# Mixer A's queries and keys projected for four heads at a time

## The chip, the cores and the metric

The kernel runs on one core of a Trainium2 chip. The metric is the device time of one execution in microseconds (us). Five engines take part: TensorE (PE, matmuls and transposes, with its own weight loads PEld), VectorE (DVE), ScalarE (ACT), GpSimd (POOL) and SyncE (SP), which here issues nearly every DMA. Each engine works through its own list of instructions in order; semaphores tie the lists together.

## The reference, cut to what matters

One layer of a streaming encoder, run for 1024 prompt frames and 32 sample frames with shared weights. The kernel puts them side by side as T = 1056 rows of x with 1024 channels: nine tiles of rows, eight of 128 and one of 32. What the change touches is the first lines of `project_inputs`:

```
h = rmsnorm(x, g_mix)
z = einsum('bld,de->ble', h, w_in)
q_a, k_a, v_a, q_i, k_i, w_i, q_b, k_b, v_b, gate_a, gate_b = split(z, ...)
q_a = rope(rmsnorm(q_a.reshape(B, L, 8, 64), g_qn), pos)    # 8 heads of 64
k_a = rope(rmsnorm(k_a.reshape(B, L, 8, 64), g_kn), pos)    # also an output
```

Mixer A (sparse attention over the 256 keys that an indexer picks) uses these queries and keys; mixer B (stick-breaking attention) has its own. Gates, an output projection and a feed-forward block follow. All of it is float32; the kernel reaches that accuracy by splitting each operand into a high and a low float32r part and adding three products (high by high, high by low, low by high).

## The kernel before, in words

All instructions are recorded first and put in order by a planner (`Plan`): each has a rank (FAST, PREP, MAIN, FILL, SLOW) and an estimated duration, and the planner walks a clock over the five engines, giving each engine next the ready instruction of the best rank, the earlier recorded one first. Since every instruction is issued by the planner, all of them carry one line, L408, in the profile; groups are told apart by their tiles. Names end in numbers in the order lists; the profile leaves these out.

The stage that changes begins at about 279 us and ends when the attention of the first heads starts, at about 488 us. In it stand:

- `project_a(p)`, rank MAIN, for p = 0 to 3, two heads at a time: 256 columns of weights (128 of queries, 128 of keys). Four weight blocks (`w_qka[p, j]`, 128 x 512 each, holding two channel blocks of 256 columns) are loaded into `wst`, cast to the high part `wh` on ACT and subtracted to the low part `wl` on POOL. For each tile of rows s, 24 matmuls (8 channel blocks k by 3 products) put 128 x 256 into a bank `s` of PSUM, of which there are three; x is the stationary operand, the weights move. ACT squares the bank into `sq`, DVE sums it into `ss`, and DVE multiplies the bank by the rope tables `tabc` and `tabs` into `ta` and `tb`, which POOL adds into `qk`. After all nine tiles comes a chain of small DVE operations (`f`, `rv`, `rw`) for the norms, then transposes of `qk` into banks `t`, their split into `az`, and stores to DRAM (`dq`, `dk`, and the output `out_k_a`).
- `project_v(p)`, inside `project_a`: two weight blocks `w_va`, 72 matmuls of rank FILL into banks `pj` (chunks of 512, 272 and 272 columns), a scaling to `vt`, transposes, and stores `dv`.
- `gate(e)` for e = 2, 3, 4 (`w_g`, 72 FILL matmuls each, scaled to `gz`, stored to `dg`).
- the top-k search of the indexer, rank SLOW, on DVE and ACT: rounds of counting (`junk`, `cnta`, `cntb` from `score` and `cand`) and, at its end, the masks (`pen`, `eq`, `pre`, `mask`).

FILL matmuls take PE whenever no MAIN matmul is ready. The weight blocks of all of these share one ring of five `wh`/`wl` pairs (WB) and three `wst`: a block can only be cast when PE is through with the block five before it. Four blocks of `w_qka[0]` are loaded ahead (`early`), while gates 0 and 1 run. `rope_tables` loads two rope tables (`ropec`, `ropes`) and multiplies them by the two norm weights into `tabc` and `tabs`, each `[128, 9, 2, 64]`.

Of the kernel before, what the change touches and what calls it, by code (L numbers as in the profile page):

```python
# [416 lines left out]
class Layer:  # L417
# [15 lines left out]
    def unit(self, src):  # L433

        nc = self.nc
        key = (src.tensor.name, src.offset)
        if key in self.begun:
            return self.begun.pop(key)
        with nc.rank(PREP):
            st = nc.tile(self.wpool, [128, 512], F32, "wst", bufs=3)  # L440
            h = nc.tile(self.wpool, [128, 512], F32R, "wh", bufs=WB)
            l = nc.tile(self.wpool, [128, 512], F32R, "wl", bufs=WB)
            nc.sync.dma_start(st, src)
            self.split(h, l, st)
# [50 lines left out]
    def run(self):  # L495
# [80 lines left out]
        for p in range(4):  # L576
            self.project_a(p)
# [356 lines left out]
    def rope_tables(self):  # L934
# [15 lines left out]

# [51 lines left out]
    def project_a(self, p):  # L1002
        nc, pr, a = self.nc, self.pr, self.a
        units = [self.unit(a["w_qka"][p, j]) for j in range(4)]
        qk = nc.tile(pr, [128, NT, 4, HD], F32, "qk", bufs=1)
        ss = nc.tile(pr, [128, NT, 4], F32, "ss", bufs=2)
        nc.gpsimd.memset(qk[:, NEW], 0.0)
        nc.gpsimd.memset(ss[:, NEW], 0.0)
        for s in range(NT):
# [3 lines left out]
            for k in range(KB):  # L1013
                xh, xl = self.x_of(k, ts_)
                wh, wl = (u[:, (k % 2) * 256:(k % 2) * 256 + 256] for u in units[k // 2])
                nc.tensor.matmul(ps[:m, :256], xh, wh, start=k == 0, stop=False)
                nc.tensor.matmul(ps[:m, :256], xh, wl, start=False, stop=False)
                nc.tensor.matmul(ps[:m, :256], xl, wh, start=False, stop=k == KB - 1)
            sq = nc.tile(pr, [128, 4, HD], F32, "sq", bufs=1)
            if p < SUMS:  # L1020
                nc.scalar.activation(sq[:m], ps[:m, :256].rearrange("p (h e) -> p h e", e=HD), AF.Square)
                nc.vector.reduce_sum(ss[:m, s], sq[:m], axis=AX.X)
            else:
                for h in range(4):
                    nc.scalar.activation(
# [595 lines left out]
```

## Time and profile before

| | us |
|---|---|
| median of 3 timed runs | 1769.09 (1766.96 to 1771.07) |
| profiled execution, first to last instruction (span) | 1767.0 |
| PE busy in it | 1739.5 |
| the stage from 279 to 488 us: PE busy | 207.27 of 209.00 |
| the same: DVE, ACT, POOL busy | 182.41, 127.33, 83.11 |

The profiled execution is as long as the fastest timed run, 1766.96, so nothing of note lies around its span. Durations of matmuls in the profile overlap (they are pipelined); how long one takes out of PE's time is read from the starts of a row of equal ones.

### The profile page before, as it was taken

What the parts mean: (1) busy time and instruction counts of PE and PEld (TensorE: products, weight loads), DVE (VectorE), ACT (ScalarE), POOL (GpSimd) and SP (SyncE); (2) the same over time, 40 slices, a digit from 0 to 9 for tenths busy, and PEclk for the clock granted to TensorE, in tenths of its full rate; (3) what the DMA queues carried; (4) which work ended last, traced back from release to release, by engine and by line L of the source; (5) the groups of instructions that cost most, each with busy time, mean ns of one, the idle gap of its engine ahead of it and who ended that gap; (6) DMA issues with size and microseconds to landing.
All of it is one profiled execution on the core that took longest, in us unless ns stands there. A gap on an engine that the chain in (4) does not pass through costs nothing.

```text
span 1767.0 us, 32459 instructions
## 1 busy us (share of the span) xinstructions
PE 1739.5 (98%) x11394; PEld 1600.1 (91%) x11394; DVE 1175.5 (67%) x2427; ACT 932.7 (53%) x2007; POOL 1054.6 (60%) x901
## 2 busy tenths in 40 slices
PE   8999999999999999999999999999999999999999
PEld 7999999999899888888888888888899999999999
DVE  7555678999666645788975556333357897777764
ACT  7444598973255676766655545432236543333331
POOL 3623232435366574899875555675558986666663
PEclk9999999999999999999999999999999999999999
DMA  8244451544566668555254353433374333333312
GB/s 258 72 133 118 116 177 59 148 144 143 178 179 168 169 183 225 175 163 151 69 162 123 118 154 98 144 109 99 106 237 137 95 104 92 94 91 96 96 48 88
DMA packets 152851, 234.90 MB, mean 133 GB/s; under 512 B 27248, under 2 KB 54480, under 8 KB 152688
## 3 DMA queue, kind: packets, MB, share of 16 engines
q1 hardware_dynamic: 152256, 232.48, 45.8%
q8 instruction: 90, 1.47, 0.4%
q14 instruction: 73, 0.60, 0.1%
q10 hardware_dynamic: 432, 0.34, 0.1%
HBM read 182.58 MB, written 50.08 MB: 132 GB/s over the span
## 4 chain that ended last, share of the span: by engine, by line
PE 85%; DVE 6%; DMA 4%; POOL 3%; issue 1%; ACT 1%; SPq 0%; ACTq 0%; POOLq 0%; DVEq 0%
PE pj L408 53%; PE s L408 13%; PE pd L408 10%; PE t L408 4%; PE o L408 4%; DMA q<-dq 1%; POOL wl L408 1%; DVE xl L408 1%; DMA k<-dk 1%; DVE raw L408 1%; DVE acc L408 1%; DVE rw L408 0%; DMA o<-do 0%; SPq L408 0%; POOL acc L408 0%
## 5 line engine op out<-in xcount | busy, mean ns | idle before, releaser
L408 POOL TENSOR_TENSOR wl<-wst,wh 128x512 fp32r<-128x512 f32 x350 | 488.5, 1400 | 388.4 <-ACT wh L408 358.2
L408 PE MATMUL pj<-xh,wh 128*128 128x512 f32 (+1 forms) x1600 | 557.3, 348 | 0.6 <-DVE vt L408 0.3
L408 PE MATMUL pj<-xh,wl 128*128 128x512 f32 (+1 forms) x1600 | 557.4, 349 | 0.0
L408 PE MATMUL pj<-xl,wh 128*128 128x512 f32 (+1 forms) x1600 | 555.8, 348 | 0.0
L408 ACT CAST wh<-wst 128x512 fp32r<-128x512 f32 x350 | 216.8, 621 | 361.7 <-PE pj L408 222.0
L408 PEld LDWEIGHTS pj<-xh,wh 128*128 128x128 f32 x1600 | 301.1, 188 | 33.6 <-ACT xh L408 0.7
L408 PEld LDWEIGHTS pj<-xh,wl 128*128 128x128 f32 x1600 | 300.8, 188 | 32.7
L408 PEld LDWEIGHTS pj<-xl,wh 128*128 128x128 f32 x1600 | 301.0, 188 | 32.1
L408 PE MATMUL pd<-xh,wh 128*128 128x272 f32 x512 | 147.6, 288 | 2.0 <-DVE y L408 2.0
L408 PE MATMUL pd<-xl,wh 128*128 128x272 f32 x512 | 147.7, 288 | 0.0
L408 PE MATMUL pd<-xh,wl 128*128 128x272 f32 x512 | 147.6, 288 | 0.0
L408 DVE TENSOR_TENSOR xl<-ru,xh 128x272 fp32r<-128x272 f32 (+1 forms) x96 | 114.2, 1202 | 46.0 <-ACT xh L408 45.7
L408 DVE TENSOR_TENSOR tt<-t,tt 128x512 fp32r<-128x512 f32 (+2 forms) x168 | 100.2, 622 | 40.3 <-ACT tt L408 38.6
L408 DVE TENSOR_TENSOR_SCAN rem<-rem 128x896 f32<-128x896 f32 (+6 forms) x66 | 118.7, 1823 | 10.0 <-ACT rem L408 9.8
L408 POOL TENSOR_TENSOR p<-p,rem 128x895 f32<-128x895 f32 (+6 forms) x66 | 103.3, 1578 | 29.8 <-DVE rem L408 26.4
L408 ACT ACTIVATE junk<-score,cand 128x384 bf16<-128x384 f32 (+1 forms) x124 | 116.1, 936 | 9.3 <-DVE cand L408 7.0
L408 ACT CAST tt<-t 128x512 fp32r<-128x512 f32 (+2 forms) x168 | 84.8, 540 | 48.2 <-PE t L408 42.8
L408 DVE TENSOR_TENSOR y<-pj,y 128x512 f32<-128x512 f32 x72 | 49.6, 689 | 83.9 <-PE pj L408 83.8
L408 PE MATMUL s<-k,q 128*128 128x384 f32 (+5 forms) x384 | 95.7, 356 | 7.1 <-DMA k<-dk 2.5
L408 PE MATMUL s<-wl,xh 128*128 128x256 f32 (+1 forms) x360 | 101.8, 285 | 0.2 <-POOL wl L408 0.2
L408 PEld LDWEIGHTS o<-tt,v 128*128 128x128 f32 x640 | 93.0, 189 | 9.7 <-DVE tt L408 1.1
L408 PE MATMUL s<-wh,xh 128*128 128x256 f32 (+1 forms) x360 | 100.3, 286 | 0.9 <-DVE small L408 0.7
(245 smaller groups left out, 3963.6 us busy)
## 6 DMA issues: line engine op xcount, KB each, us to landing
wst<-w_down SPq DMA_DIRECT2D x128, 256.0 KB, 2.7
q<-dq SPq DMA_DIRECT2D x64, 256.0 KB, 5.2
wst<-w_up SPq DMA_DIRECT2D x64, 256.0 KB, 2.7
raw<-w_up SPq DMA_DIRECT2D x64, 256.0 KB, 2.8
k<-dk SPq DMA_DIRECT2D x48, 256.0 KB, 3.5
v<-dv SPq DMA_DIRECT2D x48, 256.0 KB, 3.7
wst<-w_g SPq DMA_DIRECT2D x42, 256.0 KB, 3.4
dv<-vs SPq DMA_DIRECT2D x32, 256.0 KB, 2.4
```

What stands on the lines that cost most here:

```text
L408: fn(*args, **kw)
```

## The change: what it does

`project_a` runs for p = 0 and 1, four heads at a time. Its weights come as eight blocks of 128 x 512, one for each k, holding 256 columns of queries and 256 of keys. The first four use the ring of five; the last four have a ring of their own of four pairs in the pool `proja`, which is opened when the pools of the stage before are closed. Each matmul moves 512 columns and fills a whole bank `s`. `sq`, `ta`, `tb`, `qk`, `ss` and the norm chain are twice as wide and there are half as many. The sum of squares goes by ACT and a DVE sum for all eight columns of heads where p = 0; where p = 1 so for four of them, and for the other four by ACT alone with an accumulating output, as p = 3 did before. The two `project_v` of a pass stand behind the transposes of the first and of the second pair of heads. The rope tables are loaded straight into `tabc` and `tabs`, once for each norm weight, and multiplied in place.

Where the change moves instructions, three places. The first is PE at the start of the stage, where the eight blocks are first used; `s_3785`, `s_3789`, `s_3793` are the banks of row tiles 0, 1 and 2, `wh_1860` is block 3 (loaded ahead) and `wh_3772` block 4, the first of the new ring. Before, block pairs followed each other and no block outside the four was needed:

```order
L408 MATMUL s_3779<-wh_1851,xl0_91 128x256
L408 MATMUL s_3779<-wh_1851,xh0_90 128x256
L408 MATMUL s_3775<-wl_1861,xh0_90 128x256
L408 MATMUL s_3775<-wh_1860,xl0_91 128x256
L408 MATMUL s_3775<-wh_1860,xh0_90 128x256
```

With the change:

```order
L408 MATMUL s_3793<-wh_1860,xh0_90 128x512
L408 MATMUL s_3793<-wl_1861,xh0_90 128x512
L408 MATMUL s_3793<-wh_1860,xl0_91 128x512
L408 MATMUL s_3785<-wh_3772,xh0_90 128x512
L408 MATMUL s_3789<-wh_3772,xh0_90 128x512
L408 MATMUL s_3793<-wh_3772,xh0_90 128x512
L408 MATMUL s_3785<-wl_3773,xh0_90 128x512
L408 MATMUL s_3785<-wh_3772,xl0_91 128x512
L408 MATMUL s_3785<-wh_3775,xh0_90 128x512
L408 MATMUL s_3789<-wl_3773,xh0_90 128x512
```

36 matmuls of the three tiles with blocks 0 to 3 stand ahead of `wh_3772`, and the high part of block 4 is used three times before its low part `wl_3773` is.

The second is ACT at the same time, from the cast of the fourth block loaded ahead on (`wh`; `junk` are the counting rounds of the top-k search):

```order
L408 CAST wh<-wst 128x512
L408 ACTIVATE junk,cntb_1539<-score_1339,cand 128x768
L408 ACTIVATE junk,cntb_1539<-score_1340,cand 128x896
L408 ACTIVATE junk,cnta_1534<-score_1336,cand 128x384
L408 ACTIVATE junk,cnta_1534<-score_1341,cand 128x1024
L408 ACTIVATE sq<-s 128x256
L408 ACTIVATE junk,cntb_1538<-score_1339,cand 128x768
L408 ACTIVATE junk,cntb_1538<-score_1340,cand 128x896
L408 ACTIVATE sq<-s 128x256
```

With the change:

```order
L408 CAST wh<-wst 128x512
L408 ACTIVATE junk,cntb_1539<-score_1339,cand 128x768
L408 ACTIVATE junk,cntb_1539<-score_1340,cand 128x896
L408 ACTIVATE junk,cnta_1534<-score_1336,cand 128x384
L408 ACTIVATE junk,cnta_1534<-score_1341,cand 128x1024
L408 ACTIVATE junk,cntb_1538<-score_1339,cand 128x768
L408 ACTIVATE junk,cntb_1538<-score_1340,cand 128x896
L408 ACTIVATE junk,cnta_1535<-score_1336,cand 128x384
L408 ACTIVATE junk,cnta_1535<-score_1341,cand 128x1024
L408 CAST wh<-wst 128x512 x3
L408 ACTIVATE junk,cntb_1539<-score_1339,cand 128x768
```

The squares `sq` are gone from this place, and the casts of blocks 4, 5 and 6 stand behind two whole rounds of four counting operations; before, the next cast (a block of `w_va`) stood behind seven counting operations and two squares.

The third is SP, from the last store of gate 1 on, and PE's handover from the first four heads to the second:

```order
L408 DMA dg<-gz 128x272 x2
L408 DMA wst<-w_va 128x512 x2
L408 DMA wst<-w_qka 128x512
L408 DMA ropec<-rope_c 128x576
L408 DMA ropes<-rope_s 128x576
L408 DMA gqk<-g_qk 128x128
L408 DMA wst<-w_qka 128x512 x3
```

With the change:

```order
L408 DMA dg<-gz 128x272 x2
L408 DMA wst<-w_qka 128x512 x3
L408 DMA gqk<-g_qk 128x128
L408 DMA tabc<-rope_c 128x9x64
L408 DMA tabs<-rope_s 128x9x64
L408 DMA tabc<-rope_c 128x9x64
L408 DMA tabs<-rope_s 128x9x64
L408 DMA wst<-w_qka 128x512
L408 DMA wst<-w_va 128x512 x4
```

Three blocks of `w_qka` now stand ahead of the tables, four table loads instead of two follow, and the eighth block stands behind them. PE's handover with the change (`s_3907` to `s_3915` are row tiles 0 to 2 of the second pass, `wh_3891` its block 3, `wh_3960` a block of `w_va`, `pj_3874` the last chunk of the second `project_v`):

```order
L408 MATMUL pj_3874<-xh1_92,wl_3870 128x272
L408 MATMUL s_3907<-wh_3891,xh0_90 128x512
L408 MATMUL s_3911<-wh_3891,xh0_90 128x512
L408 MATMUL s_3915<-wh_3891,xh0_90 128x512
L408 MATMUL pj_3966<-xh0_90,wh_3960 128x512
L408 MATMUL pj_3966<-xl0_91,wh_3960 128x512
L408 MATMUL s_3907<-wl_3892,xh0_90 128x512
L408 MATMUL s_3907<-wh_3891,xl0_91 128x512
```

Here both `project_v` of the first pass are done, and what PE does next waits for the casts of `wh_3891` and `wh_3960`, which take the places of the two blocks that `pj_3874` has just used. On the whole there are 1093 PE instructions in the stage instead of 1521, and PE changes between kinds of work (bank or shape) 74 times instead of 113. Within the first attention heads the order of every engine becomes the one before again, and stays so to the end.

```diff
@@ -430,16 +430,17 @@
         self.nc.scalar.copy(h, x)
         self.nc.gpsimd.tensor_sub(l, x, h.bitcast(F32))
 
-    def unit(self, src):
+    def unit(self, src, pool=None, bufs=WB):
 
         nc = self.nc
+        pool = pool or self.wpool
         key = (src.tensor.name, src.offset)
         if key in self.begun:
             return self.begun.pop(key)
         with nc.rank(PREP):
             st = nc.tile(self.wpool, [128, 512], F32, "wst", bufs=3)
-            h = nc.tile(self.wpool, [128, 512], F32R, "wh", bufs=WB)
-            l = nc.tile(self.wpool, [128, 512], F32R, "wl", bufs=WB)
+            h = nc.tile(pool, [128, 512], F32R, "wh", bufs=bufs)
+            l = nc.tile(pool, [128, 512], F32R, "wl", bufs=bufs)
             nc.sync.dma_start(st, src)
             self.split(h, l, st)
         return h, l
@@ -573,7 +574,7 @@
         nc.close(self.pr, self.ik)
         self.pr = nc.open("proja")
         self.rope_tables()
-        for p in range(4):
+        for p in range(2):
             self.project_a(p)
         with nc.rank(SLOW):
             self.top_k()
@@ -935,18 +936,16 @@
         nc, a, pr = self.nc, self.a, self.pr
         self.tc_ = nc.tile(pr, [128, NT, 2, HD], F32, "tabc")
         self.ts_ = nc.tile(pr, [128, NT, 2, HD], F32, "tabs")
-        C = nc.tile(pr, [128, NT, HD], F32, "ropec")
-        S = nc.tile(pr, [128, NT, HD], F32, "ropes")
         g = nc.tile(pr, [128, 2, HD], F32, "gqk")
-        nc.sync.dma_start(C, a["rope_c"])
-        nc.sync.dma_start(S, a["rope_s"])
         nc.sync.dma_start(g, a["g_qk"].unsqueeze(0).to_broadcast([128, 2, HD]))
         for j in range(2):
-            nc.vector.tensor_mul(self.tc_[:, :, j], C, g[:, j].unsqueeze(1).to_broadcast([128, NT, HD]))
+            C, S = self.tc_[:, :, j], self.ts_[:, :, j]
+            nc.sync.dma_start(C, a["rope_c"])
+            nc.sync.dma_start(S, a["rope_s"])
+            nc.vector.tensor_mul(C, C, g[:, j].unsqueeze(1).to_broadcast([128, NT, HD]))
             gx = g[:, j].rearrange("p (s e) -> p s e", s=2)[:, ::-1, :].unsqueeze(1).to_broadcast([128, NT, 2, 32])
-            nc.vector.tensor_mul(
-                self.ts_[:, :, j].rearrange("p t (s e) -> p t s e", s=2),
-                S.rearrange("p t (s e) -> p t s e", s=2), gx)
+            S = S.rearrange("p t (s e) -> p t s e", s=2)
+            nc.vector.tensor_mul(S, S, gx)
 
     def project_v(self, p, mixer, w, vout):
 
@@ -1001,9 +1000,9 @@
 
     def project_a(self, p):
         nc, pr, a = self.nc, self.pr, self.a
-        units = [self.unit(a["w_qka"][p, j]) for j in range(4)]
-        qk = nc.tile(pr, [128, NT, 4, HD], F32, "qk", bufs=1)
-        ss = nc.tile(pr, [128, NT, 4], F32, "ss", bufs=2)
+        units = [self.unit(a["w_qka"][p, k], *(() if k < 4 else (pr, 4))) for k in range(KB)]
+        qk = nc.tile(pr, [128, NT, 8, HD], F32, "qk", bufs=1)
+        ss = nc.tile(pr, [128, NT, 8], F32, "ss", bufs=1)
...
@@ -1012,60 +1011,62 @@
             ps = self.bank("s")
             for k in range(KB):
                 xh, xl = self.x_of(k, ts_)
-                wh, wl = (u[:, (k % 2) * 256:(k % 2) * 256 + 256] for u in units[k // 2])
-                nc.tensor.matmul(ps[:m, :256], xh, wh, start=k == 0, stop=False)
-                nc.tensor.matmul(ps[:m, :256], xh, wl, start=False, stop=False)
-                nc.tensor.matmul(ps[:m, :256], xl, wh, start=False, stop=k == KB - 1)
-            sq = nc.tile(pr, [128, 4, HD], F32, "sq", bufs=1)
-            if p < SUMS:
-                nc.scalar.activation(sq[:m], ps[:m, :256].rearrange("p (h e) -> p h e", e=HD), AF.Square)
-                nc.vector.reduce_sum(ss[:m, s], sq[:m], axis=AX.X)
-            else:
-                for h in range(4):
-                    nc.scalar.activation(
-                        sq[:m, h], ps[:m, HD * h:HD * h + HD], AF.Square, accum_out=ss[:m, s, h:h + 1])
-            ta = nc.tile(pr, [128, 256], F32, "ta", bufs=1)
-            tb = nc.tile(pr, [128, 256], F32, "tb", bufs=1)
+                wh, wl = units[k]
+                nc.tensor.matmul(ps[:m], xh, wh, start=k == 0, stop=False)
+                nc.tensor.matmul(ps[:m], xh, wl, start=False, stop=False)
+                nc.tensor.matmul(ps[:m], xl, wh, start=False, stop=k == KB - 1)
+            nh = 8 if p == 0 else 4
+            sq = nc.tile(pr, [128, 8, HD], F32, "sq", bufs=1)
+            nc.scalar.activation(
+                sq[:m, :nh], ps[:m, :nh * HD].rearrange("p (h e) -> p h e", e=HD), AF.Square)
+            nc.vector.reduce_sum(ss[:m, s, :nh], sq[:m, :nh], axis=AX.X)
+            for h in range(nh, 8):
+                nc.scalar.activation(
+                    sq[:m, h], ps[:m, HD * h:HD * h + HD], AF.Square, accum_out=ss[:m, s, h:h + 1])
+            ta = nc.tile(pr, [128, 512], F32, "ta", bufs=1)
+            tb = nc.tile(pr, [128, 512], F32, "tb", bufs=1)
             nc.vector.tensor_mul(
-                ta[:m].rearrange("p (q h e) -> p q h e", q=2, h=2),
-                ps[:m, :256].rearrange("p (q h e) -> p q h e", q=2, h=2),
-                self.tc_[:m, s].unsqueeze(2).to_broadcast([m, 2, 2, HD]))
+                ta[:m].rearrange("p (q h e) -> p q h e", q=2, h=4),
+                ps[:m].rearrange("p (q h e) -> p q h e", q=2, h=4),
+                self.tc_[:m, s].unsqueeze(2).to_broadcast([m, 2, 4, HD]))
             nc.vector.tensor_mul(
...
...
             nc.gpsimd.tensor_add(qk[:m, s].rearrange("p h e -> p (h e)"), ta[:m], tb[:m])
-        f = nc.tile(pr, [128, NT, 4], F32, "f", bufs=2)
-        rsb = self.rs.unsqueeze(2).to_broadcast([128, NT, 4])
+        f = nc.tile(pr, [128, NT, 8], F32, "f", bufs=1)
+        rsb = self.rs.unsqueeze(2).to_broadcast([128, NT, 8])
         nc.vector.tensor_mul(f, ss, rsb)
         nc.vector.tensor_mul(f, f, rsb)
         ss = f
-        f = nc.tile(pr, [128, NT, 4], F32, "f2", bufs=2)
-        self.rsqrt(f, ss, HD, lambda n: nc.tile(pr, [128, NT, 4], F32, n, bufs=1))
+        f = nc.tile(pr, [128, NT, 8], F32, "f2", bufs=1)
+        self.rsqrt(f, ss, HD, lambda n: nc.tile(pr, [128, NT, 8], F32, n, bufs=1))
         nc.vector.tensor_mul(f, f, rsb)
-        nc.vector.tensor_scalar_mul(self.fq[:, :, 2 * p:2 * p + 2], f[:, :, 0:2], HD ** -0.5)
-        nc.vector.tensor_mul(qk[:, :, 2:4], qk[:, :, 2:4], f[:, :, 2:4].unsqueeze(3).to_broadcast([128, NT, 2, HD]))
-        cols = slice(p * 128, p * 128 + 128)
+        nc.vector.tensor_scalar_mul(self.fq[:, :, 4 * p:4 * p + 4], f[:, :, 0:4], HD ** -0.5)
+        nc.vector.tensor_mul(qk[:, :, 4:8], qk[:, :, 4:8], f[:, :, 4:8].unsqueeze(3).to_broadcast([128, NT, 4, HD]))
+        cols = slice(p * 256, p * 256 + 256)
         for sl in GROUPS:
             o = self.o["k_a"][128 * sl[0]:128 * sl[-1] + rows(sl[-1]), cols]
             m = rows(sl[0])
             nc.sync.dma_start(
                 o.rearrange("(t r) e -> r t e", r=m),
-                qk[:m, sl[0]:sl[-1] + 1, 2:4].rearrange("p t h e -> p t (h e)"))
...
+                qk[:m, sl[0]:sl[-1] + 1, 4:8].rearrange("p t h e -> p t (h e)"))
+        for i in range(2):
+            for j, dst in ((0, self.dq), (1, self.dk)):
+                h = 4 * j + 2 * i
+                for sl in GROUPS:
+                    n = sum(rows(s) for s in sl)
+                    pt = self.bank("t")
+                    for c, s in enumerate(sl):
+                        m = rows(s)
+                        nc.tensor.transpose(
+                            pt[:, c * 128:c * 128 + m], qk[:m, s, h:h + 2].rearrange("p h e -> p (h e)"),
+                            self.ident[:m, :m])
+                    zz = nc.tile(pr, [128, 2, 512], F32R, "az", bufs=2)
+                    nc.scalar.copy(zz[:, 0, :n], pt[:, :n])
+                    nc.vector.tensor_sub(zz[:, 1, :n], pt[:, :n], zz.bitcast(F32)[:, 0, :n])
+                    self.keep(dst, 4 * p + 2 * i, slice(128 * sl[0], 128 * sl[0] + n), zz)
+            self.project_v(2 * p + i, 0, a["w_va"], self.o["v_a"])
 
 
     def softmax_weights(self, parts, L, mask, f, p):
@@ -1558,9 +1559,8 @@
         qi[:, 256:].reshape(4, 2, 128, NI_B).transpose(0, 2, 1, 3).reshape(4, 128, 512))
     out["w_qb"], out["w_kb"], out["w_vb"], out["w_va"] = units(qb), units(kb), units(vb), units(va)
     out["w_g"] = units(np.concatenate([ga, gb], axis=1))
-    qk = np.concatenate([qa.reshape(D, 4, 128), ka.reshape(D, 4, 128)], axis=2)
-    out["w_qka"] = np.ascontiguousarray(
-        qk.reshape(4, 2, 128, 4, 256).transpose(3, 0, 2, 1, 4).reshape(4, 4, 128, 512))
+    qk = np.concatenate([qa.reshape(D, 2, 256), ka.reshape(D, 2, 256)], axis=2)
+    out["w_qka"] = np.ascontiguousarray(qk.reshape(KB, 128, 2, 512).transpose(2, 0, 1, 3))
     out["w_ba"], out["w_bb"], out["w_out"] = units(f["w_branch_a"]), units(f["w_branch_b"]), units(f["w_out"])
     out["w_up"], out["w_down"] = units(f["w_up"]), units(f["w_down"])
     out["g_mix"] = np.ascontiguousarray(f["g_mix"].reshape(KB, 128).T)
```

More of the change, by code (lines that the diff above doesn't have):

```diff
@@ L1032, in project_a @@
-                self.tc_[:m, s].unsqueeze(2).to_broadcast([m, 2, 2, HD]))
+                ta[:m].rearrange("p (q h e) -> p q h e", q=2, h=4),
+                ps[:m].rearrange("p (q h e) -> p q h e", q=2, h=4),
+                self.tc_[:m, s].unsqueeze(2).to_broadcast([m, 2, 4, HD]))
             nc.vector.tensor_mul(
-                tb[:m].rearrange("p (q h s e) -> p q h s e", q=2, h=2, s=2),
-                ps[:m, :256].rearrange("p (q h s e) -> p q h s e", q=2, h=2, s=2)[:, :, :, ::-1, :],
@@ L1036, in project_a @@
-                self.ts_[:m, s].rearrange("p q (s e) -> p q s e", s=2).unsqueeze(2).to_broadcast([m, 2, 2, 2, 32]))
+                tb[:m].rearrange("p (q h s e) -> p q h s e", q=2, h=4, s=2),
+                ps[:m].rearrange("p (q h s e) -> p q h s e", q=2, h=4, s=2)[:, :, :, ::-1, :],
+                self.ts_[:m, s].rearrange("p q (s e) -> p q s e", s=2).unsqueeze(2).to_broadcast([m, 2, 4, 2, 32]))
             nc.gpsimd.tensor_add(qk[:m, s].rearrange("p h e -> p (h e)"), ta[:m], tb[:m])
-        f = nc.tile(pr, [128, NT, 4], F32, "f", bufs=2)
@@ L1053, in project_a @@
                 o.rearrange("(t r) e -> r t e", r=m),
-                qk[:m, sl[0]:sl[-1] + 1, 2:4].rearrange("p t h e -> p t (h e)"))
-        for j, dst in ((0, self.dq), (1, self.dk)):
-            for sl in GROUPS:
-                n = sum(rows(s) for s in sl)
-                pt = self.bank("t")
-                for i, s in enumerate(sl):
-                    m = rows(s)
-                    nc.tensor.transpose(
-                        pt[:, i * 128:i * 128 + m], qk[:m, s, 2 * j:2 * j + 2].rearrange("p h e -> p (h e)"),
-                        self.ident[:m, :m])
-                zz = nc.tile(pr, [128, 2, 512], F32R, "az", bufs=2)
-                nc.scalar.copy(zz[:, 0, :n], pt[:, :n])
-                nc.vector.tensor_sub(zz[:, 1, :n], pt[:, :n], zz.bitcast(F32)[:, 0, :n])
-                self.keep(dst, 2 * p, slice(128 * sl[0], 128 * sl[0] + n), zz)
-        self.project_v(p, 0, a["w_va"], self.o["v_a"])
+                qk[:m, sl[0]:sl[-1] + 1, 4:8].rearrange("p t h e -> p t (h e)"))
[15 more added lines that the diff above has]
+            self.project_v(2 * p + i, 0, a["w_va"], self.o["v_a"])
     def softmax_weights(self, parts, L, mask, f, p):
```

## The prediction

> **What bounds the kernel now.** First the page's busy times and the clock, then the wide windows of the stage that changes, then PE's own waits in it.
>
> ```profile
> span 1767.0 us, 32459 instructions
> PE 1739.5 (98%) x11394; PEld 1600.1 (91%) x11394; DVE 1175.5 (67%) x2427; ACT 932.7 (53%) x2007; POOL 1054.6 (60%) x901
> PEclk9999999999999999999999999999999999999999
> ...
> 279.00:488.00 209.00, 207.27 (x1524) 195.04 (x1523) 182.41 (x515) 127.33 (x339) 83.11 (x83) 1.00 0.48 141
> ...
> PE s L408 <- DVE small L408: 0.7, 1, 0.7
> PE pj L408 <- DVE vt L408: 0.3, 1, 0.3
> PE s L408 <- POOL wl L408: 0.2, 1, 0.2
> PE s L408 <- ACT sq L408: 0.2, 1, 0.2
> PE t L408 <- POOL qk L408: 0.2, 1, 0.2
> ```
>
> PE is the bound at full clock. In the 209 us of the stage (windows: length, then busy time of PE, PEld, DVE, ACT, POOL, then clock) it is idle for 1.7 us, and the wait rows name five single waits for them, 1.6 us together. So time leaves this stage only with PE work, and comes back only with a PE wait. DVE is next with 182 of 209 us, so what it waits for must be asked too.
>
> **The matmuls.** 864 of 256 columns become 432 of 512. How long one takes is read from the starts of unbroken rows of equal ones.
>
> ```profile
> 278.99 0.28 PE L408 MATMUL s<-wh,xh 128*128 128x256 f32 x1
> ...
> 373.96 0.60 PE L408 MATMUL t<-ident,vt 128*128 128x128 f32 x4
> 374.31 0.36 PE L408 MATMUL s<-wh,xh 128*128 128x256 f32 x1
> ...
> 388.68 0.28 PE L408 MATMUL s<-wh,xh 128*32 128x256 f32 x1
> 391.43 0.49 PE L408 MATMUL t<-ident,qk 128*128 128x128 f32 x3
> ...
> 468.08 0.40 PE L408 MATMUL pj<-xh,wh 128*128 128x512 f32 x1
> 473.58 0.28 PE L408 MATMUL pj<-xh,wh 128*128 128x272 f32 x1
> 479.61 0.40 PE L408 MATMUL pj<-xh,wh 128*128 128x512 f32 x1
> 485.11 0.28 PE L408 MATMUL pj<-xh,wh 128*128 128x272 f32 x1
> ...
> 487.78 0.41 PE L408 MATMUL s<-k,q 128*128 128x384 f32 x1
> ```
>
> From 374.31 to 388.68 stand five row tiles of 24 matmuls: 14.37 us / 120 = 0.1198 us. The tile of 32 rows follows, 24 in 2.75 us: 0.1146. One chunk of 512 columns is 24 matmuls: 468.08 to 473.58 and 479.61 to 485.11 are 5.50 us each: 0.2292. So a pair of narrow ones takes 0.2396 and one wide one 0.2292: 0.0104 less. Over 768 / 2 = 384 pairs that is 4.0 us; the 48 pairs of the small tile, taken alike, give at most 0.5 (2 x 0.1146 = 0.2292 says nothing is left; I take 0.2). **Term 1: -4.2 us.** The bounds are -4.5 and, should the wide ones in the banks `s` cost just two narrow ones, 0. I stay near the measured step, since the two kinds already differ only in which operand is x.
>
> [...]
>
> **The breaks.** The steps of one kind of work do not add up to the stage. Between 278.99 (its first matmul) and 487.78 (the first of attention) lie 208.8 us. With the steps above, 6.03 us / 48 = 0.1256 for 272 columns (473.58 to 479.61), and 0.35 / 4 = 0.0875 for a transpose (373.96 to 374.31), its 1521 instructions come to 768 x 0.1198 + 96 x 0.1146 + 192 x 0.2292 + 357 x 0.1256 + 108 x 0.0875 = 92.0 + 11.0 + 44.0 + 44.8 + 9.4 = 201.2. So 7.6 us are lost, 1.6 of them in the five waits; the other 6.0 lie, I take it, at the 113 changes from one bank or shape to another, 0.053 us each. The new order has 74. **Term 2: 39 x 0.053 = -2.1 us,** with 0 as the other bound, should the loss lie elsewhere.
>
> **New waits of PE.** The weights of eight blocks do not fit the ring of five, so block 4 is cast after the stage has begun.
>
> ```profile
> 269.16 0.93 ACT L408 ACTIVATE junk<-score,cand 128x768 bf16<-128x768 f32 x1
> 273.40 0.94 ACT L408 ACTIVATE junk<-score,cand 128x768 bf16<-128x768 f32 x1
> 277.61 0.62 ACT L408 CAST wh<-wst 128x512 fp32r<-128x512 f32 x1
> 278.13 0.93 ACT L408 ACTIVATE junk<-score,cand 128x768 bf16<-128x768 f32 x1
> 278.31 1.29 POOL L408 TENSOR_TENSOR wl<-wst,wh 128x512 fp32r<-128x512 f32 x1 [7.88 <-ACT wh L408]
> 273.89 6.09 SPq L408 DMA_DIRECT2D dg<-gz  x3
> 280.07 1.38 SPq L408 DMA_DIRECT2D wst<-w_va  x2
> wst<-w_qka SPq DMA_DIRECT2D x12, 256.0 KB, 2.8
> ropec<-rope_c SPq DMA_DIRECT2D x1, 288.0 KB, 5.1
> ropes<-rope_s SPq DMA_DIRECT2D x1, 288.0 KB, 5.3
> out_k_a<-qk SPq DMA_DIRECT2D x8, 256.0 KB, 2.8
> dv<-vs SPq DMA_DIRECT2D x8, 16.0 KB, 1.7
> 289.25 0.75 DVE L408 TENSOR_TENSOR tabc<-ropec,gqk 128x576 f32<-128x576 f32 x1
> ```
>
> At the start: PE begins at 278.99 as before, and 36 wide matmuls reach to 278.99 + 36 x 0.2292 = 287.2, when it wants `wh_3772`. The block's load stands where `w_va` was issued, 280.07, and lands 2.8 us later, 282.9. ACT reaches its cast after two sets of four counting operations (4.24 us a set, 269.16 to 273.40) from 278.13: 286.6, done 287.2. POOL's part takes 1.29: 288.5. PE has spent three matmuls by then (287.9): a wait of 0.6. Blocks 5 and 6 follow at POOL's pace, 1.29, while PE takes seven matmuls, 1.6 us, per block: no wait. Block 7 needs the `wst` that POOL frees at 288.5, lands at about 291.5, is cast after the next set (three casts at 0.52, 277.61 to 278.13, end at 288.2; + 4.2 = 292.4), high part at 293.0, low part at 294.3; PE wants these 25 and 32 matmuls after 287.8: 293.5 and 295.1. So 0.6, with what the first wait before (0.7) gone.
>
> At the handover to the second four heads (the last order list) PE has used up both `project_v`. Block 3 of the second pass takes the place of a block that PE leaves 1.5 us (12 x 0.1256) before; cast and subtraction take 0.6 + 1.3, with three high products (0.7) and two of `w_va` (0.5) in front: no wait if ACT is free, 1 us if it has just begun a counting operation. Block 6 of the same pass stands on SP behind two `dv` stores, which wait for ACT and DVE: 0 to 2 us. When the second pass ends, a block of `w_va` waits on POOL behind an addition to `qk`: 0 to 2. Behind a waiting PE stand the transposes too, and for these ACT and DVE with `az` and `vs`, none of which PE needs soon. Altogether 0.6 to 5.6; I take 2.5, since the old order met three such handovers with 0.2 to 0.3 each. The old 1.6 go. **Term 3: +0.9.**
>
> **The tables.** Four loads instead of two, in pieces of 256 B where they were 2304 B. `out_k_a` moves 512 pieces of 512 B in 2.8 us, against 1.7 for the smallest `dv` store: at most (2.8 - 1.7) / 512 = 2 ns a piece, 2.5 us for 1152 pieces, 10 for four tables. Issued from 281.8 on, they land between 288 (the two took 5.1 and 5.3) and 293. DVE reaches them at about 288, where it stood at 289.25 with three sums of 0.41 in front that are now gone. `ta` and `tb` of row tile 0 can start only when its bank is full, 34 matmuls after 287.8: 295.6; PE wants that bank 14 matmuls later, at 298.8. Behind the tables hang DVE's next round, then two counting operations and `sq` on ACT, some 6 us together, which free that bank too; so tables complete at 292 are early enough, and **term 4 is 0**, +1 if they come at 293. [...]
>
> **The other engines.**
>
> ```profile
> L408 DVE TENSOR_TENSOR ta<-s,tabc 128x256 f32<-128x256 f32 x32 | 13.2, 413 | 0.6 <-POOL qk L408 0.4
> L408 DVE TENSOR_TENSOR vt<-pj,rb 128x512 f32<-128x512 f32 x4 | 2.7, 684 | 0.9 <-PE pj L408 0.9
> L408 DVE TENSOR_REDUCE ss<-sq 128x4 f32<-128x256 f32 x24 | 9.8, 410 | 0.2
> 460.00:480.00 20.00, 20.00 (x135) 18.59 (x134) 9.13 (x19) 3.97 (x9) 5.51 (x5) 1.00 0.48 157
> 466.62 0.63 POOL L408 TENSOR_SCALAR mask<-pre 32x544 bf16<-32x544 f32 x1 [3.25 <-PE pj L408]
> 480.69 0.38 SPq L408 DMA_DIRECT2D k<-dk  x1
> ```
>
> DVE gets 36 wide products (0.684, as `vt`) for 72 narrow ones (0.413): -5.1 us; the sums stay about equal (27 x 0.41 = 11.1 against 9 x 0.68 + 9 x 0.41 = 9.8). This work lies under PE and is worth nothing by itself. It matters only as cover: the top-k search ends with the last mask at 467.2, 13 us before attention's first load at 480.69, and that load waits for a store of gate 4 that PE feeds. So the end of the stage follows PE, and from there on the order is the same.
>
> **The sum.** -4.2 - 2.1 + 0.9 + 0 = -5.4: a span of 1767.0 - 5.4 = 1761.6. The profiled execution lies 2.1 us below the median of the runs; I put the change on the median: 1769.1 - 5.4 = **1763.7 us**.
>
> **Rivals.** What a measurement of this kernel can tell from no change is about 0.2%, 3.5 us.
>
> ```profile
> ACT vs L408 <- DMA dv<-vs: 7.7, 2, 6.0
> ```
>
> - *The waits eat it* (0.23): every handover costs its upper end, 5.6 us less the old 1.6. -4.2 - 2.1 + 4.0 = -2.3: 1766.8. For it: blocks pass ACT behind counting operations and SP behind stores. Against it: five waits of at most 0.7 before, under the same rules.
> - *No fixed part saved* (0.08): a wide matmul in the banks `s` costs two narrow ones, term 1 is 0, and -2.1 + 0.9 = -1.2: 1767.9. The step rows speak against it. [...]
> - *PE runs dry* (0.06), slower: at the handover to the second four heads nothing is left for PE but these blocks. If one `dv` store holds SP there as such a store held ACT for 6.0 us, block 6 is late by that, and ACT misses its turn by one counting set, 4.2: +10.2 at this one place, in all -4.2 - 2.1 + 0.9 + 10.2 = +4.8: 1773.9. From an added wait of 5.4 on the change loses.
> - *The tables come late* (0.03): pieces twice as slow as my upper bound, 20 us for four, complete at 302; 6 us later, at 308, PE gets the bank it wants at 298.8: +9.2 - 5.4 = +3.8: 1772.9.
>
> That the work is not moved as the change says is ruled out by the order lists.
>
> **The numbers.** The forecast has 0.60. Its own range is -8 to -3: with term 3 at -1 (only the first wait left) -7.3 and a little for the runs, with term 3 at +3 -3.3. Of its 0.60 all but 0.02 lies below -3.5, and 0.04 of the first rival: faster 0.62. The rest of these two (0.02 + 0.19), the second rival and 0.02 of the last are no change: 0.31; slower 0.07. Eight times in ten the time should lie between -9 and 0 from the median: 1760.0 to 1769.0.
>
> **What the new profile would show.** Wide `s` matmuls 0.229 apart in unbroken rows (0.240: no saving). PE in the stage busy some 203 us, attention's first matmul near 482.4 instead of 487.8. One PE wait of about 0.6 for POOL `wl` near 288. Waits above 2 us on `s` for ACT `wh` or POOL `wl` near the second pass would carry the first rival, one above 5 the third. DVE held by a table load past 292 would carry the last. Wrong I would be on term 2 if the difference of the spans were smaller than term 1 with waits no longer than before.

## The result and the profile after

| | before | after |
|---|---|---|
| median of 4 timed runs, us | 1768.95 (1766.96 to 1771.07) | 1791.98 (1791.6 to 1794.14) |
| profiled span, us | 1767.0 | 1790.2 |
| first matmul of the stage to first matmul of attention, us | 208.8 | 231.6 |

The change makes the kernel slower: the ratio is 1.0132 (95% interval 1.0118 to 1.0146), some 23 us. The stage is 22.9 us longer and the span 23.2, so nearly all of it arises in the stage that was changed. I had forecast 5.4 us less. One execution among all that follow, of run 8, ran in a slower state of the chip (1883.32 us at a granted clock of 0.851) and is left out of that run's median and ratio.

The time of an execution is not its span: the profiled one after the change took 1792.01 us with a span of 1790.2, and the runs below show 1.7 to 1.9 us, run 11 2.1 to 2.2. So the span before, 1767.0, was wrongly set beside the fastest time, 1766.96, as if nothing lay around it. The forecast was put on the median and does not hang on this.

First the page of the changed kernel (busy times, and the granted clock in 40 slices), then windows of its stage (length, then busy time of PE, PEld, DVE, ACT, POOL, then clock, DMA share and GB/s), then what PE waited for between 279 and 512 us:

```profile
span 1790.2 us, 31437 instructions
PE 1747.2 (98%) x10962; PEld 1582.6 (88%) x10962; DVE 1176.1 (66%) x2360; ACT 932.4 (52%) x1996; POOL 1046.8 (58%) x879
PEclk9999999999899999999999999999999999999999
...
300.00:350.00 50.00, 50.00 (x247) 39.71 (x246) 47.07 (x144) 43.16 (x87) 20.14 (x16) 1.00 0.18 53
350.00:400.00 50.00, 43.29 (x217) 35.41 (x216) 38.74 (x126) 42.20 (x120) 12.24 (x10) 0.93 0.58 174
400.00:430.00 30.00, 30.00 (x138) 22.66 (x138) 26.02 (x46) 7.90 (x48) 12.68 (x10) 1.00 0.12 38
430.00:470.00 40.00, 28.99 (x148) 25.04 (x147) 36.47 (x56) 8.01 (x23) 12.46 (x10) 0.79 0.55 171
470.00:510.00 40.00, 40.00 (x257) 36.58 (x258) 16.51 (x30) 8.56 (x18) 9.59 (x8) 1.00 0.58 173
...
PE t L408 <- DVE az L408: 6.0, 5, 2.8
PE s L408 <- ACT az L408: 3.7, 1, 3.7
PE t L408 <- DVE vs L408: 3.5, 2, 2.1
PE pj L408 <- DVE vt L408: 2.1, 3, 1.0
PE t L408 <- DVE qk L408: 2.0, 1, 2.0
PE s L408 <- POOL wl L408: 0.4, 1, 0.4
PE s L408 <- ACT wh L408: 0.3, 1, 0.3
PE pj L408 <- ACT wh L408: 0.2, 1, 0.2
```

Where row tiles follow each other, PE is busy (300 to 350, 400 to 430 us). It runs dry twice: at the end of the first four heads (350 to 400) and, worse, at the end of the second (430 to 470), and both times the granted clock falls too (0.93 and 0.79, against 1.00 in the other three windows). The waits are for `az`, `vs`, `vt` and `qk`, that is, for work that takes the transposes away; for weight blocks (`wl`, `wh`) PE waits 0.8 us in all. Behind 470 us PE is fully busy for 40 us: work that could have filled the holes was still there.

Why it did not fill them is seen in the timeline of the second hole (start, duration, engine, instruction; in brackets the idle time before it and what ended it):

```profile
445.70 2.55 DVE L408 TENSOR_TENSOR qk<-qk,f 128x2304 f32<-128x2304 f32 x1
...
446.13 0.28 PE L408 MATMUL pj<-xh,wl 128*128 128x272 f32 x1
...
448.39 1.06 PE L408 MATMUL t<-ident,qk 128*128 128x128 f32 x8 [1.98 <-DVE qk L408]
...
450.42 0.24 PE L408 MATMUL t<-ident,qk 32*128 32x32 f32 x1 [0.96 <-DVE az L408]
...
453.13 0.75 DVE L408 TENSOR_TENSOR vs<-t,vs 128x256 fp32r<-128x256 f32 x2
453.79 1.08 DVE L408 CUSTOM_DVE_ANT_0 pen<-pen,score 128x896 f32<-128x896 f32 x1
454.02 0.37 PE L408 MATMUL t<-ident,vt 128*32 128x128 f32 x1 [2.11 <-DVE vs L408]
...
455.65 0.18 ACT L408 CAST az<-t 128x32 fp32r<-128x32 f32 x1 [3.05 <-DMA dk<-az]
455.85 1.15 DVE L408 TENSOR_SCALAR_CACHE_REDUCE junk<-score,lowb 128x896 bf16<-128x896 f32 x1
456.92 0.18 DVE L408 TENSOR_TENSOR az<-t,az 128x32 fp32r<-128x32 f32 x1
457.16 1.11 PE L408 MATMUL t<-ident,vt 128*128 128x128 f32 x4 [2.77 <-DVE az L408]
458.39 1.03 DVE L408 TENSOR_TENSOR vt<-pj,rb 128x512 f32<-128x512 f32 x2
459.12 0.59 PE L408 MATMUL pj<-xh,wh 128*128 128x272 f32 x1 [0.85 <-DVE vt L408]
```

At 446.13 PE ends the second chunk of the second `project_v` of the pass. Its two chunks fill both banks `pj`. They can leave only for `vt`, which has one buffer and still holds the values of the first `project_v`; and these leave only by transposes, which stand behind those of `qk`, which waited for the end of the norm chain (DVE, 2.55 us, over at 448.25). From there on the drain is one chain: a bank `t`, ACT's copy, DVE's subtraction, a store, the next bank. On DVE the links stand among the steps of the top-k search (here `pen` 1.08 and `junk` 1.15 us); on ACT the 3.05 us before one `az` were spent on its store. Only when the last transposes of `vt` have been issued can DVE write it anew (458.39) and PE get a bank `pj` (459.12). For these 13 us the three gates, 216 matmuls, were still to come, and none had a bank to go to. Before the change each pass had one `project_v`, and the row tiles of the next pass, or the gates, followed it.

The first hole has the same lack of banks, from another side:

```profile
372.40 0.61 ACT L408 CAST wh<-wst 128x512 fp32r<-128x512 f32 x1
...
390.39 0.28 PE L408 MATMUL pj<-xh,wl 128*128 128x272 f32 x1
390.61 0.24 PE L408 MATMUL t<-ident,qk 32*128 32x32 f32 x1
390.92 0.52 POOL L408 MEMSET qk<- 128x512 f32 x1 [16.54 <-PE t L408]
...
394.05 0.68 DVE L408 TENSOR_TENSOR tb<-s,tabs 128x512 f32<-128x512 f32 x1
394.62 0.16 ACT L408 CAST az<-t 128x32 fp32r<-128x32 f32 x1
394.88 0.77 PE L408 MATMUL s<-wh,xh 128*128 128x512 f32 x1 [3.73 <-ACT az L408]
...
422.81 1.65 ACT L408 CAST wh<-wst 128x512 fp32r<-128x512 f32 x3
...
426.37 0.48 PE L408 MATMUL pj<-xh,wh 128*128 128x512 f32 x1
```

The third `project_v` stops half-way at 390.39 with both banks `pj` begun and goes on at 426.37: its second weight block is cast only at 422.81 (no cast falls between 372.40 and there), as four of the five places of the common ring belong to blocks of the row tiles until the pass ends. And the row tiles stand too, since `qk` has one buffer: POOL may clear and refill it only after its last transpose (390.61), which stood late in the same queue for the banks `t`, for `az` and for `vs`, and a bank `s` comes free with the end of `tb`, 394.73. The bracket names `az`, which ended 0.05 us later; the two are too close to be told apart. This hole is read from the trace alone; no run gives `qk` a second buffer.

### The profile page after: what moved, and what is told of

It is laid out like the page before. It is cut to its first block, busy times and chain, and to the rows that moved or that the text cites. A ratio compares the mean times of both kernels' runs of the same rounds, so it can differ in the third digit from the quotient of the medians.

```text
span 1790.2 us, 31437 instructions
## 1 busy us (share of the span) xinstructions
PE 1747.2 (98%) x10962; PEld 1582.6 (88%) x10962; DVE 1176.1 (66%) x2360; ACT 932.4 (52%) x1996; POOL 1046.8 (58%) x879
## 4 chain that ended last, share of the span: by engine, by line
PE 81%; DVE 9%; DMA 3%; issue 2%; ACT 2%; POOL 2%; SPq 0%; ACTq 0%; POOLq 0%; DVEq 0%
PE pj L408 52%; PE s L408 11%; PE pd L408 10%; PE t L408 4%; PE o L408 4%; DVE junk L408 1%; DMA q<-dq 1%; DVE xl L408 1%; ACT junk L408 1%; POOL wl L408 1%; DVE rw L408 1%; DVE raw L408 1%; DVE acc L408 1%; SPq L408 0%; DVE ta L408 0%
## 5 line engine op out<-in xcount | busy, mean ns | idle before, releaser
L408 ACT CAST wh<-wst 128x512 fp32r<-128x512 f32 x350 | 216.3, 620 | 356.6 <-PE pj L408 226.0
L408 DVE TENSOR_TENSOR_SCAN rem<-rem 128x896 f32<-128x896 f32 (+6 forms) x66 | 120.1, 1841 | 11.8 <-ACT rem L408 10.7
L408 DVE TENSOR_TENSOR y<-pd,y 128x272 f32<-128x272 f32 x128 | 53.9, 435 | 71.0 <-PE pd L408 71.0
L408 PE MATMUL o<-tt,v 128*128 128x256 f32 (+1 forms) x640 | 99.7, 278 | 0.6 <-ACT wh L408 0.5
```

The source lines that it names most:

```text
L408: fn(*args, **kw)
```

## The experiments

Two rivals stand beside this theory: that the wide form itself (banks, blocks, wide DVE work) holds PE up, and that the search on DVE and ACT does it alone. In the table stand all runs; the ratio is to the kernel before, run beside each; "stage" runs from the first matmul of the stage to attention's first, the waits are PE's idle times in it that the trace names, and "behind" runs from attention's first matmul to the last instruction. The last three columns come from the one profiled execution of each run.

| run | median us | ratio (95%) | stage us | waits us | behind us |
|---|---|---|---|---|---|
| before | 1768.95 | | 208.8 | 1.7 | 1279.2 |
| after | 1791.98 | 1.0132 (1.0118 to 1.0146) | 231.6 | 18.1 | 1278.7 |
| 1 before, `project_v` in pairs | 1800.78 | 1.0171 (1.0147 to 1.0195) | 239.9 | 24.0 | 1279.2 |
| 2 after, narrow matmuls | 1791.9 | 1.0117 (1.0093 to 1.0141) | 231.1 | 18.4 | 1279.5 |
| 3 after, short search | 1778.82 | 1.0046 (1.0033 to 1.0059) | 220.4 | 10.1 | 1276.6 |
| 4 before, short search | 1774.67 | 1.0022 (1.0009 to 1.0035) | 212.9 | 5.1 | 1281.6 |
| 5 after, rings of 5 and 3 | 1789.38 | 1.0115 (1.0089 to 1.014) | 224.8 | 14.9 | 1283.3 |
| 6 = 5, two `vs` | 1779.14 | 1.0052 (1.0033 to 1.007) | 219.0 | 10.7 | 1278.9 |
| 7 = 5, `vt` in halves | 1777.64 | 1.0047 (1.0035 to 1.006) | 222.7 | 10.3 | 1277.8 |
| 8 = 5, 6 and 7 | 1773.79 | 1.0018 (1.0006 to 1.0031) | 215.3 | 7.8 | 1274.9 |
| 9 = 8, last `project_v` later | 1767.76 | 0.999 (0.9978 to 1.0002) | 210.2 | 4.6 | 1275.4 |
| 10 = 9, fifth block early, sums by DVE | 1765.56 | 0.9984 (0.9975 to 0.9993) | 207.9 | 3.5 | 1274.9 |
| 11 before, two `vs`, `vt` in halves | 1770.07 | 1.0012 (1.0002 to 1.0021) | 209.5 | 3.0 | 1279.7 |
| 12 = 5, tables as before | 1790.5 | 1.0121 (1.0104 to 1.0138) | 226.0 | 14.7 | 1284.0 |

**1: the pairs without the width.** In the kernel before:

```diff
-        self.project_v(p, 0, a["w_va"], self.o["v_a"])
+        for q in range(p - 1, p + 1) if p % 2 else ():
+            self.project_v(q, 0, a["w_va"], self.o["v_a"])
```

> The kernel before (256 columns, two heads a pass, old tables), with one edit: the four project_v are recorded in pairs, 0 and 1 behind the second pass, 2 and 3 behind the fourth. Theory 1 (two project_v in a row: the second fills both banks pj, its vt has one buffer which the transposes of the first still hold, so no FILL matmul can run and PE waits for the drain through t, vs and DVE): slower by 10 to 30 us, PE waits on t and pj for DVE vs, vt and az in two places, with a granted clock below 1 behind the longest. Theory 2 (the wide banks, their eight weight blocks and the wide DVE work hold PE up): within 3 us of the kernel before. Theory 3 (the top-k search stands ahead of what PE needs on DVE and ACT): 0 to 5 us slower.

It is 30 us slower (0.0171 of 1770), at the upper end of what theory 1 said, with narrow matmuls and the old tables. PE's waits between 279 and 512 us:

```profile
PE t L408 <- DVE az L408: 10.4, 5, 4.8
PE s L408 <- DVE small L408: 5.0, 1, 5.0
...
PE t L408 <- DVE vs L408: 2.0, 2, 1.6
```

The drain's names, as after the change. The 5.0 us for `small` are another matter: they fall at 293.89, in the first pass, where with the edit no `project_v` is there as a filler. Another 2.7 us fall on `s` for `tb`. So the pairs alone, without any width, bring a loss as large as the change's, with the same names; not all of these 30 us are the drain.

**2: the width without its matmuls.** In the changed kernel:

```diff
-            for k in range(KB):
+            for k, c in ((k, slice(c, c + 256)) for c in (0, 256) for k in range(KB)):
                 xh, xl = self.x_of(k, ts_)
-                wh, wl = units[k]
-                nc.tensor.matmul(ps[:m], xh, wh, start=k == 0, stop=False)
+                wh, wl = (z[:, c] for z in units[k])
+                nc.tensor.matmul(ps[:m, c], xh, wh, start=k == 0, stop=False)
...
```

> The changed kernel with its matmuls narrow again: each row tile gets 48 matmuls of 256 columns, first the left half of the bank, then the right, all else as changed. Theory 1: as slow as the changed kernel, 1788 to 1798 us, since the pairs of project_v stay; 4 us more PE work, part of it hidden in the waits. Theory 2, if it is the width of a matmul: back to about 1770.

1791.9: as slow as the changed kernel. Halving the matmuls again does not give the time back. The planner ordered this kernel anew, and 4.2 of its 18.4 us of waits are on `s` for ACT `wh`; so the run clears the width of a matmul, while the eight blocks and the full banks stayed. Blocks and banks are cleared by runs 9 and 10, which have them too, with rings of five and three.

**3 and 4: the search cut short,** in both kernels:

```diff
-        for b in range(30, -1, -1):
+        for b in range(30, 22, -1):
```

> The changed kernel with 8 bit rounds of the top-k search instead of 31, so that the masks, and the attention output with them, are others; read against the kernel before with the same cut. Theory 3: the difference of the two is -6 to 0 us, since DVE and ACT are then free when PE needs them. Theory 1: 5 to 15 us are left, since vt, vs and the stores are passed one after the other with idle engines too; waits on t and pj stay, most for vs and vt.

> The kernel before with 8 bit rounds of the top-k search instead of 31 (other masks, other attention output), as the measure for the run above. All theories: 1762 to 1772 us, since PE is the bound in this stage and waited for 1.6 us only.

The difference between the two is 4.2 us instead of 23, which neither theory had: less than theory 1's 5 to 15, more than theory 3's 0. In the stage alone it is 7.5 us (220.4 and 212.9); behind the stage the changed kernel is 5 us shorter here, for a reason that stays open. The kernel before did not stay within my range either: it is 0.22% slower with the short search (waits of 5.1 us; the planner arranged it anew), and why is open too. Two windows of the changed kernel with the short search:

```profile
350.00:400.00 50.00, 44.86 (x227) 37.34 (x226) 27.26 (x42) 14.63 (x61) 17.02 (x12) 0.90 0.57 171
...
430.00:470.00 40.00, 35.76 (x211) 32.03 (x210) 16.27 (x33) 8.96 (x22) 7.74 (x6) 0.91 0.68 212
```

DVE is busy for 27 of 50 and 16 of 40 us now, and PE still stands for 5.1 and 4.2 us in the same two places. So the drain makes waits even with engines that have time to spare, and with the whole search between its links they are almost twice as long (18.1 and 10.1 us). Nor is the search enough by itself: with the `project_v` apart, the same full search left PE of the kernel before with 1.7 us of waits.

**5 to 8: the drain widened.** Two buffers for `vs` need 4 KB a partition, which comes from the weight blocks (run 5); `vt` is split without more space (run 7); run 8 has both.

```diff
-        units = [self.unit(a["w_qka"][p, k], *(() if k < 4 else (pr, 4))) for k in range(KB)]
+        units = [self.unit(a["w_qka"][p, k], *(() if k < 5 else (pr, 3))) for k in range(KB)]
...
-            vs = nc.tile(pr, [128, 2, 4, 128], F32R, "vs", bufs=1)
+            vs = nc.tile(pr, [128, 2, 4, 128], F32R, "vs", bufs=2)
...
-        vt = nc.tile(pr, [128, T], F32, "vt", bufs=1)
+        vts = [nc.tile(pr, [128, 512], F32, "vta"), nc.tile(pr, [128, T - 512], F32, "vtb")]
```

> The changed kernel with five blocks in the common ring and three in the own one, instead of four and four. It frees 4 KB a partition on chip, which the next runs need, and is their measure. It gives the blocks to project_v later by one ring place. Theory 1: the pairs of project_v stay as they are: 1786 to 1796 us. If the blocks' rings were what holds PE up (my first and third rival): a change of more than 5 us to either side.

> The run above with two buffers for vs instead of one, so that a group of value transposes can be drained while the stores dv of the one before still read. Theory 1 with vs as the link that paces the drain (each of its three groups waits for copy, subtraction and store of the one before): 6 to 14 us faster than the run above. If the drain is paced by vt or the transposes of qk alone: within 3 us of it.

> The ring run with vt as two tiles, columns 0 to 511 and 512 to 1055, in the same space, so that the second project_v can put its first chunk away as soon as the first four transposes of the first are done; one more store of v_a. Theory 1 with vt as the link on which the banks pj wait: the waits on pj for DVE vt shorten and FILL matmuls run between the transposes: 4 to 12 us faster than the ring run. If vt only names who came last: within 3 us.

> Both of the last two edits on the ring run. Theory 1: the gains add to 12 to 22 us, so 1768 to 1780 us, with the granted clock of the stage back above 0.98. Theory 2 (the wide form itself is slow): no more than 5 us faster than the changed kernel.

Run 5 is about as slow as the change, but for two reasons that nearly cancel: its stage is 6.8 us shorter, and behind the stage it takes 4.6 us longer. So the rings do have a part in the stage, with 14.9 us of waits instead of 18.1 and 13.7 us at half clock instead of 23.9. Behind the stage PE's order in runs 5, 7 and 12 differs from the one before as far as 1140 us, while in runs 6 and 8 it is the same from attention's first matmul on.

On run 5, two `vs` give 10.2 us, the split of `vt` 11.7, both 15.6: within the bounds of theory 1, and not of the rivals. But part of this is not the drain. In the stage alone two `vs` give 5.8 us, just under theory 1's 6, and both edits 9.5; the rest lies behind the stage. (The profile of run 7 is its slowest execution, 1782.60, so its stage says little.) The changed kernel is the better measure for run 6, since the two take the same time behind the stage: ring and two `vs` take 12.7 us out of the stage, and with `vt` split 16.4 are gone. The two edits do not add, as one would expect of two that loosen the same chain. All of this is buffers and rings; no instruction of the wide form was touched.

**9 and 10: the order, and the start.** Run 9 records the last `project_v` behind gate 2, so that the banks `pj` go to a gate while the third drains; run 10 loads a fifth block early and sums the squares of all eight heads on DVE.

```diff
-            self.project_v(2 * p + i, 0, a["w_va"], self.o["v_a"])
+            if (p, i) != (1, 1):
+                self.project_v(2 * p + i, 0, a["w_va"], self.o["v_a"])
...
             self.gate(e)
+            if e == 2:
+                self.project_v(3, 0, a["w_va"], self.o["v_a"])
...
-        self.early(*(a["w_qka"][0, j] for j in range(4)))
+        self.early(*(a["w_qka"][0, j] for j in range(5)))
...
-            nh = 8 if p == 0 else 4
+            nh = 8
```

> The run with both edits (two vs, vt in halves, ring of five and three), and the fourth project_v recorded behind gate 2 instead of right behind the third, so that the banks pj go to a gate whose result nothing holds while the third drains. Theory 1: the wait on pj for DVE vt of the second pass goes: 2 to 5 us faster than that run, 1768 to 1773 us. If that run is now held by DVE's work alone: within 2 us of it.

> The run above with two more edits: a fifth weight block is loaded ahead, into the common ring, and the sums of squares of the second four heads go like those of the first, by ACT in one operation and a DVE sum for all eight heads, without the four accumulating operations of ACT. Theory 1 with PE as the bound once more: what is saved is the waits at the start (about 2 us) and those behind ACT sq and DVE tb, so 1762 to 1769 us, for the first time not above the kernel before. If the wide form had saved nothing of PE's work: 1768 to 1773.

> The kernel before with the same two edits on buffers (two vs, vt in halves), everything else as before. All theories: 1765 to 1771 us, since its project_v stand 36 us apart and PE waited for 1.6 us in this stage. It is the measure for the two runs above: if it gains as much as they do, the wide form has no part in it.

Run 9 is about 5 us faster than run 8 (0.28% by the ratios), the waits on `pj` for `vt` are gone from its trace, and it is level with the kernel before. Run 10 is 0.16% faster than the kernel before (0.9984, 0.9975 to 0.9993), the one version here that beats both kernels. Of the 5.5 us between the two profiled spans (1761.5 and 1767.0) only 0.9 lie in the stage; 4.3 lie behind it, where PE waits 12.5 us instead of 14.4 and the stretch of half clock that the kernel before shows from 1413.7 us on, for 3.41 us, is missing (the profiled execution of run 10 has a mean granted clock of 1.0). So the lead of run 10 cannot be put down to the wide form alone. The kernel before with the same buffers (run 11) gains nothing, 1.0012 (1.0002 to 1.0021). Whether the kernel before would also gain from run 10's sums by DVE was not tried, nor the later `project_v` without the buffers. The windows of run 10 and its waits:

```profile
350.00:400.00 50.00, 48.25 (x246) 39.73 (x246) 43.63 (x138) 40.98 (x93) 14.29 (x12) 1.00 0.52 156
...
430.00:470.00 40.00, 39.46 (x258) 35.55 (x257) 36.48 (x57) 10.03 (x25) 13.10 (x10) 1.00 0.72 223
...
PE s L408 <- ACT az L408: 1.7, 1, 1.7
PE s L408 <- ACT sq L408: 1.3, 1, 1.3
PE t L408 <- DVE qk L408: 0.5, 1, 0.5
```

DVE does as much between 430 and 470 us as after the change (36.48 and 36.47), and PE stands 0.5 us instead of 11.0. What was late was never DVE's total, but the order in which PE could hand its banks on.

**12: the tables.** Run 5 with the loads into `ropec` and `ropes` and the products into `tabc` and `tabs` as they were before.

```diff
-            C, S = self.tc_[:, :, j], self.ts_[:, :, j]
-            nc.sync.dma_start(C, a["rope_c"])
-            nc.sync.dma_start(S, a["rope_s"])
-            nc.vector.tensor_mul(C, C, g[:, j].unsqueeze(1).to_broadcast([128, NT, HD]))
+            nc.vector.tensor_mul(self.tc_[:, :, j], C, g[:, j].unsqueeze(1).to_broadcast([128, NT, HD]))
```

> The ring run (five and three) with the rope tables as before: loaded once each into ropec and ropes and multiplied into tabc and tabs, which just fits into the 4 KB. If the loads in place or their smaller pieces are late for PE (my last rival): 2 to 9 us faster than the ring run's 1789. If not (term 4 at 0): within 3 us of it, with some 2 us less DVE work before 300 us.

1790.5 beside 1789.4: the tables in place cost nothing that can be measured. DVE's work between 279 and 300 us is 0.5 us less (18.70 and 19.17), not 2.

## Why the prediction was wrong, step by step

**Term 1, matmul steps (-4.2 us): right in kind, too large.** Rows of the changed kernel, five row tiles without a break, and where the small tile begins:

```profile
300.27 0.50 PE L408 MATMUL s<-wh,xh 128*128 128x512 f32 x1
...
328.19 0.39 PE L408 MATMUL s<-wh,xh 128*32 128x512 f32 x1
...
511.51 0.59 PE L408 MATMUL s<-k,q 128*128 128x384 f32 x2
```

27.92 us / 120 = 0.2327, where I had taken 0.2292 from the banks `pj`. A pair of narrow ones took 0.2396, so 0.0069 is saved, not 0.0104: 384 x 0.0069 = 2.6 us. The small tile saves nothing (24 in 5.53 us, 0.2304, against 2 x 0.1146). The saving is real all the same: taking the waits out, run 10's stage is 207.9 - 3.5 = 204.4 us, the kernel before's 208.8 - 1.7 = 207.1, 2.7 less. In run 9 it is 210.2 - 4.6 = 205.6, 1.5 less, with six more matmuls `pj` (0.8 us) ahead of attention than in run 10.

**Term 2, breaks (-2.1): nothing seen of it.** These 1.5 to 2.7 us are used up by term 1, and so is the account of the change (below). The 6.0 us that I had put down to changes of bank or shape did not shrink with their number, in these two comparisons.

**Term 3, new waits (+0.9): this is the step that failed.** What it costed came out: `wl` of block 4 held PE for 0.4 us at 289.41 (0.6 forecast), the blocks at the handover for 0.4, at 367.18 and 368.30 (0 to 3 forecast). What it dismissed did not: "Behind a waiting PE stand the transposes too, and for these ACT and DVE with `az` and `vs`, none of which PE needs soon." PE needed them for its next bank. I had written in the description of the change that both `project_v` of a pass now stand behind its transposes, and never asked what the second one finds there: `vt` full, `vs` and `qk` single, `pj` two; nor that blocks which serve a whole pass of 50 us would hold four of five ring places against the blocks of `project_v`. The account: waits 18.1 instead of 1.7, +16.4; slower matmuls and transposes behind them +8.9, nearly all of it the clock (last section); term 1 -2.6. Together +22.7, and the stage grew by 22.9.

"The other engines" failed with it: DVE's 5.1 us were called worth nothing since they "lie under PE". PE was the bound of the stage only as long as some matmul had a free bank; the cover was the row tiles and gates, and these were shut out.

**Term 4, tables (0): right** (run 12). **The rivals.** *PE runs dry* had the side, and its threshold of 5.4 us of added wait was passed threefold, but its mechanism was wrong: block 6 behind a `dv` store was not late. I had looked for it among the weight blocks alone. The signs I named for the first and third rival, waits on `s` for `wh` or `wl` above 2 us, did not appear; the long ones are on `t`, and the one on `s` is for `tb`.

## What to carry to other kernels

When work is grouped more coarsely, count the buffers along the way out, not only the instructions: two producers that follow each other directly share each single buffer and each pair of PSUM banks, and the second fills the banks until the first has drained through every link. Filler work is worth something only if it has a bank to go to; so ask of each filler which ring it needs and who holds that ring while the bound engine waits. Where such a wait is found, spacing the producers and a second buffer at the slowest link can be enough: 4 KB and a changed order took 21.5 us out of the stage here (231.6 to 210.2), while taking most of the search from DVE and ACT, which changes the masks, took out 11.2 (run 3, 220.4).

## What the runs showed of the hardware that I had not expected

The clock. 1-us windows of the changed kernel (columns as above):

```profile
431.00:432.00 1.00, 0.00 (x0) 0.00 (x0) 0.97 (x3) 0.84 (x2) 0.76 (x3) 1.00 0.00 0
432.00:433.00 1.00, 0.21 (x1) 0.13 (x1) 1.00 (x3) 0.00 (x0) 1.00 (x1) 1.00 0.00 0
433.00:434.00 1.00, 0.90 (x7) 0.90 (x8) 1.00 (x4) 0.26 (x1) 0.19 (x1) 1.00 0.27 70
434.00:435.00 1.00, 1.00 (x7) 1.00 (x7) 1.00 (x2) 0.00 (x0) 0.00 (x0) 0.61 0.94 201
435.00:436.00 1.00, 1.00 (x7) 1.00 (x6) 1.00 (x2) 0.62 (x1) 0.16 (x1) 0.50 1.01 285
...
437.00:438.00 1.00, 1.00 (x7) 0.95 (x7) 0.87 (x2) 0.15 (x1) 0.12 (x1) 0.68 0.92 315
...
464.00:465.00 1.00, 1.00 (x7) 1.00 (x6) 0.03 (x1) 0.20 (x1) 0.84 (x1) 0.53 0.00 0
```

A hole of 2 us (one 32-column transpose in it) is followed by a granted clock of 0.50 from 434.2 on, when PE had been busy again since 433.10, and for some 3.4 us; in the long hole it falls at 451.3 and stays at 0.50 until 464.9, 5.8 us after PE's matmuls began again at 459.12. At half clock a matmul of 512 columns took 0.43 us (394.88 to 400.12), one of 272 took 0.23. Worked out at full-clock steps (0.2327, 0.1257 and, for a transpose, 0.0875), four stretches lost 2.6 us (394.88 to 400.12), 1.6 (433.10 to 437.74), 2.1 (18 transposes from 448.39 to 459.12, waits left out) and 2.6 (459.12 to 464.73): 8.9 us, about half as much as the waits themselves. Of the transposes' 2.1 us, 0.6 fall before 451.3, at full clock, so some 8 us are the clock's.

In its stage the changed kernel has three such stretches, of 6.83 us (393.26 to 400.08), 3.41 (434.22 to 437.63) and 13.65 (451.28 to 464.93), the kernel before none. Whether one comes is not settled in these runs by the length of the wait alone. The same wait of 2.5 to 2.7 us, on `s` for `tb` near 300 us, stands in runs 5 to 9 and 12. In runs 6, 7, 8 and 12 the clock goes to half for 3.41 us within 0.8 us of its end (0.70, 0.72, 0.57 and 0.61 from 299 to 303 us); in runs 5 and 9 it stays at 1.00.

In the changed kernel the half clock ended 5.2 us after PE's first matmul behind the wait (394.88 to 400.08), 4.5 us (433.10 to 437.63) and 5.8 us (459.12 to 464.93).
